# Convolution taps as scaled copies on ScalarE, summed in whole tiles, and one more seven-product unit pair in the first panel pair of two down parts

## The chip, the cores and the metric

The kernel runs on one core of a Trainium2 chip. The metric is the device time of one execution in microseconds: 2241.81 us is the median of three runs before the change (2240.89 to 2243.47). A core has TensorE (matmuls, with weight loads that overlap them), VectorE (DVE), ScalarE (ACT) and GpSimd (POOL) for arithmetic, SyncE (SP), which here only issues transfers, and 16 DMA engines. Each engine works through its own list of instructions in the order written.

## The reference, cut to what matters

The model is a two-layer trunk on 256 tokens of width 2048. Each layer has an attention part and a channel mixer; the change lies in the mixer, a gated MLP with a causal depthwise convolution of width 3 between the up-projection and the activation:

```python
def causal_dwconv(u, w, b):
    s_ = u.shape[1]
    up = jnp.pad(u, ((0, 0), (CONV_WIDTH - 1, 0), (0, 0)))
    return w[0] * up[:, 0:s_] + w[1] * up[:, 1:s_ + 1] + w[2] * up[:, 2:s_ + 2] + b

def conv_ffn(h, w_up, conv_w, conv_b, w_down):
    u = causal_dwconv(h @ w_up, conv_w, conv_b)
    a, val = split_cols(u, [FFN_HIDDEN, FFN_HIDDEN])
    return (jax.nn.silu(a) * val) @ w_down
```

FFN_HIDDEN is 5632, so `w_up` is 2048 x 11264 and `w_down` 5632 x 2048.

## The kernel before, in words

**Products.** Every float32 operand is split into a high part that TensorE takes at full pace (type fp32r) and a low part, the rest. A product is then three matmuls: high x high, low x high (both with the high weights, `whi`) and high x low (`wlo`). Weights arrive in units of 128 x 1024 words: two row blocks of 128 (chunks) by 512 output columns. `split_unit` loads a unit on SyncE's queue into `raw` (four buffers), casts it on ScalarE to `whi` (L208, three buffers) and subtracts on VectorE to get `wlo` (L217, three buffers). A plain unit is 12 matmuls: two token blocks of 128, two chunks, three each.

**Panels.** A panel is 512 output columns. `proj_tm` runs one panel through all its units, `proj_two` two panels. Evacuation copies the sums from PSUM, which has four accumulator banks.

**Seven products.** `proj_seven` takes two panels at a time. For a unit pair (the same two chunks in both panels) listed in its `forms` it computes the 2 x 2 block product with seven block products in place of eight, 21 matmuls in place of 24. It needs sums of the weight blocks, made on VectorE as they arrive (L346 to L349, then casts L314 and subtractions L315), and sums of the activation blocks, the `forms` tiles, made by `token_sums` (L400 to L406). Unit pairs that are not listed run as plain ones.

**The mixer.** The hidden width is worked through in three parts of 16, 16 and 12 chunks (`PARTS`). In each part up panels come first: one panel gives two chunks of the gate and two of the value, so a part has 8, 8 and 6 panels. Then the down-projection multiplies the part's chunks by `w_down` and adds to `x`. In the first two parts it runs as two panel pairs through `proj_seven`, each with eight unit pairs. `SEVEN` lists their seven-product places, counted from 0: (3, 5) in the first pair and (3, 5, 7) in the second. The last part has none: `proj_two`, then two `proj_tm`.

**The convolution.** An up panel's sums leave PSUM through ScalarE (L1116) token by token. VectorE transposes squares (L438), a write to DRAM and four reads back on ScalarE's queue (L446) bring them into `u` as channel by token, with two zero columns in front. `taken(j, base, u, i)` then handles half i of the panel, one gate and one value chunk of 128 x 256: ScalarE starts each with the last tap and the bias (L1092), VectorE adds the two other taps (L1093, L1094), ScalarE applies Silu (L1096), VectorE multiplies (L1097), and `split` makes the high and low parts in `m` (L523, L524), which the down-projection reads. For the panels whose chunks are a seven-product unit pair, `summed` makes the token sums.

**Order.** The steps after an evacuation are hung on the units that follow: `later((3, write), (6, read), (8, taken 0), (9, taken 1))` counts `split_unit` calls (in a seven-product unit pair, its two `passed()` calls), and each step is issued after the newest cast. For the second panel of a layer the last two counts are two higher. Loads, casts and subtractions of weights carry a higher priority than the rest (`AHEAD`); within these bounds a planner with a model of the instructions' times writes the order for each engine.

**Last panel.** The last up panel of a part gives the chunks of the last unit of the down panels. Its steps run while the down-projection is already under way.

Of the kernel before, what the change touches and what calls it, by code (L numbers as in the profile page):

```python
# [12 lines left out]
F32 = mybir.dt.float32  # L13
F32R = mybir.dt.float32r
I32 = mybir.dt.int32
AF = mybir.ActivationFunctionType
ALU = mybir.AluOpType
PSUM = bass.MemoryType.PSUM

P = 128  # L20
T = 256
# [10 lines left out]
PARTS = ((0, 16), (16, 32), (32, 44))  # L32
# [4 lines left out]
NVER = 96  # L37
NUNIT = 1024
AHEAD = 300
SEVEN = ((3, 5), (3, 5, 7))  # L40
LAST = ()

SPREAD = [128 * q + 32 * k + i for k in range(4) for i in range(32) for q in range(4)]
# [94 lines left out]
def _trunk(ctx: ExitStack, tc: tile.TileContext, xt, xtok, memt, wp, wgu, gns, gfin, cnv, par, msk, out):  # L138
    nc = tc.nc
    where, _ = _layout()  # L140
    V, S, TE = nc.vector, nc.scalar, nc.tensor
# [36 lines left out]
    def later(*steps):  # L178

        for units, step in steps:  # L180
            due.append([units, step])
# [242 lines left out]
    def natural(v):  # L424
        return v.rearrange("p (t h) -> p t h", h=2)
# [23 lines left out]
    def back():  # L449
        return tp.tile([P, 4, T], F32, name="back", tag="back", bufs=2)  # L450
# [65 lines left out]
    def split(dst, i, src, g=None, dealt=True):  # L516

        hi, lo = dst[i][:, 0, :], dst[i][:, 1, :]
        if dealt:
            hi, lo = (v.rearrange("p (h t) -> p h t", h=2) for v in (hi, lo))  # L520
            src = src.rearrange("p (t h) -> p h t", h=2)
        if g is None:
            S.activation(hi, src, AF.Copy)  # L523
            V.tensor_tensor(lo, src, hi.bitcast(F32), ALU.subtract)  # L524
        else:
            S.activation(hi, src, AF.Copy, scale=g)
            V.scalar_tensor_tensor(lo, src, g, hi.bitcast(F32), ALU.mult, ALU.subtract)  # L527
# [535 lines left out]
    def ffn(l, nx, h, m, then, ending=None):  # L1063
        with tc.tile_pool(name=f"ffn{l}", bufs=1) as fp, ExitStack() as ends:
# [3 lines left out]
            sp = sums.enter_context(tc.tile_pool(name=f"sums{l}", bufs=1))  # L1068
            cw = fp.tile([P, 4 * 88], F32, name="cw")
            nc.sync.dma_start(cw, cnv[l])  # L1070
            us = [fp.tile([P, 4, T + 2], F32, name=f"u{i}") for i in range(2)]
            for u in us:
                nc.gpsimd.memset(u[:, :, :2], 0.0)
            turn = [0]
            tiles = [sp.tile([P, 2, 4, P], F32R, name=f"forms{i}") for i in range(3)]
            held = []

            def spare_tile(name, dtype):
# [2 lines left out]
            def form(t):  # L1081
                return lambda i: [t[:, h, i, :] for h in range(2)]

            def taken(j, base, u, i):

                cv = []
                for c in range(2):
                    v = u[:, 2 * c + i, :]
                    col = (c * 44 + j + i) * 4
                    w = [cw[:, col + n : col + n + 1] for n in range(4)]  # L1090
                    r = fp.tile([P, T], F32, name=f"cv{c}", tag=f"cv{c}", bufs=3)
                    S.activation(r, v[:, 2:], AF.Identity, bias=w[3], scale=w[2])  # L1092
                    V.scalar_tensor_tensor(r, v[:, 1 : T + 1], w[1], r, ALU.mult, ALU.add)  # L1093
                    V.scalar_tensor_tensor(r, v[:, :T], w[0], r, ALU.mult, ALU.add)  # L1094
                    cv.append(r)
                S.activation(cv[0], cv[0], AF.Silu)  # L1096
                V.tensor_tensor(cv[1], cv[0], cv[1], ALU.mult)  # L1097
                split(m, j + i - base, cv[1])
                if (j - base) // 2 in parts[base]:
                    held.append(cv[1])  # L1100
                    if i:
                        summed(parts[base][(j - base) // 2])

            def summed(form):
                ab = [natural(h)[:, :, b] for h in held for b in range(2)]
                held.clear()
                token_sums(*ab, sp.tile([P, 4, P], F32, name="sf", tag="sf"), [form[:, h, :, :] for h in range(2)])

            def panel(j, base, slack=0):
                held = []  # L1110

                def evac(b, a):
                    if not held:
                        held.append(Turn("turned"))
                    e = tp.tile([P, 512], F32, name="scaled", tag="scaled", bufs=2)
                    S.activation(e, a, AF.Copy, scale=nx.col()[:, b : b + 1])  # L1116
                    held[0].put(b, e)
                    if not b:
                        return
                    u = us[turn[0] % 2]  # L1120
                    turn[0] += 1
                    later((3, held[0].write), (6, lambda: held[0].read(lambda k: u[:, k, 2:])),
                          (8 + slack, lambda: taken(j, base, u, 0)), (9 + slack, lambda: taken(j, base, u, 1)))

                return evac

            parts = {lo: dict(zip(SEVEN[1] if p < len(PARTS) - 1 else LAST, tiles)) for p, (lo, _) in enumerate(PARTS)}
            for p, (lo, hi) in enumerate(PARTS):
                forms = parts[lo]
                js = list(range(lo, hi, 2))  # L1130
# [6 lines left out]
                if p < len(PARTS) - 1:  # L1137
                    for f, at in zip((0, 2), SEVEN):
                        add_seven(key, f, m, {u: form(forms[u]) for u in at}, spare_tile)
# [33 lines left out]
    n, then, _ = preparing("ffn0", bufB)  # L1173
# [4 lines left out]
    n, then, _ = preparing("ffn1", bufA)  # L1178
# [132 lines left out]
```

## Time and profile before

| | value |
|---|---|
| median of three runs | 2241.81 us (2240.89 to 2243.47) |
| span of the profiled execution | 2241.1 us |
| TensorE busy | 2227.2 us, 99%, 10267 matmuls |
| VectorE busy | 1658.5 us, 74% |
| ScalarE busy | 1294.0 us, 58% |
| DMA | 516.98 MB, mean 231 GB/s |
| granted TensorE clock | 0.999 |

The page and the views come from one execution, taken by the hardware profiler; the span is the time from its first to its last instruction, and the page gives no other time for that execution. The timed runs are others. Busy time of TensorE includes the overlap of neighbouring matmuls (a 128 x 512 one is shown with about 0.39 us though one starts every 0.227 us in the mixer), so its share says that it hardly pauses, and the pace is read from starts. Views used: the page, the list of what each engine waited for, groups of instructions by line and shape (busy us, mean ns of one, then idle time before them and what ended it), busy time by stretch, and instructions in order of time (start us, duration us, engine, line, count).

### The profile page before, as it was taken

The page shows a single profiled execution, that of the slowest core. Times are in us where ns is not written, and L with a number is a line of the kernel's source. Part 1 is how long each engine was busy: PE and PEld are TensorE (multiplying, and loading weights), DVE is VectorE, ACT ScalarE, POOL GpSimd, SP SyncE. Part 2 cuts the span into 40 slices and gives each one's busy share as a digit, 9 for nine tenths or more (in the row PEclk, how much of TensorE's full clock was granted, in tenths as well). Part 3 has the DMA queues.
Part 4 walks back from the last instruction along what each step waited for, and adds up shares of the span by engine and source line. Part 5 has one row for each costly group of instructions (what it writes and reads, how often), then busy time and mean ns, then how long its engine had stood idle before and what let it go on. Part 6 is the DMA issues. An engine that isn't in the chain of part 4 may idle for free.

```text
span 2241.1 us, 29637 instructions
## 1 busy us (share of the span) xinstructions
PE 2227.2 (99%) x10267; PEld 1860.8 (83%) x10267; DVE 1658.5 (74%) x2608; ACT 1294.0 (58%) x1921; POOL 44.6 (2%) x71
## 2 busy tenths in 40 slices
PE   9999999999999999999999999999999999999998
PEld 7888888888888888888888898888888888888886
DVE  7568887667689677886777875666778967787766
ACT  7555665656565465555656655555665555554654
POOL 0000000000000000000000000000000000000000
PEclk9999999999999999999999999999999999999999
DMA  9875667677875778667778777677876677767784
GB/s 319 277 234 188 205 208 224 202 234 242 256 222 201 243 233 249 213 203 246 235 254 263 243 239 222 196 233 244 255 243 220 204 239 244 240 193 233 237 242 150
DMA packets 276894, 516.98 MB, mean 231 GB/s; under 512 B 149884, under 2 KB 158600, under 8 KB 276616
## 3 DMA queue, kind: packets, MB, share of 16 engines
q1 hardware_dynamic: 124296, 427.24, 58.9%
q10 hardware_dynamic: 149760, 80.51, 12.6%
q0 software_dynamic: 2688, 7.34, 1.1%
q8 instruction: 80, 1.31, 0.2%
q14 instruction: 70, 0.57, 0.1%
HBM read 470.44 MB, written 44.58 MB: 230 GB/s over the span
## 4 chain that ended last, share of the span: by engine, by line
PE 95%; DMA 3%; DVE 1%; issue 1%; ACT 0%; SPq 0%; DVEq 0%; ACTq 0%
PE acc L229 24%; PE acc L230 24%; PE acc L233 24%; PE acc L291 16%; PE ps_s L291 1%; DMA back<-xturned 1%; PE ps_o L291 1%; PE ps_t L291 1%; DMA back<-turned 1%; DMA raw<-wp 1%; PE ps_s L833 0%; DMA turned<-square 0%; PE ps_s L634 0%; PE ps_t L623 0%; PE ps_o L645 0%
## 5 line engine op out<-in xcount | busy, mean ns | idle before, releaser
L217 DVE TENSOR_TENSOR wlo<-raw,whi 128x1024 fp32r<-128x1024 f32 (+4 forms) x763 | 912.6, 1199 | 458.0 <-ACT whi L208 429.5
L208 ACT ACTIVATE whi<-raw 128x1024 fp32r<-128x1024 f32 (+4 forms) x763 | 791.2, 1040 | 704.7 <-PE acc L230 471.9
L229 PE MATMUL acc<-whi,B 128*128 128x512 f32 (+3 forms) x1440 | 548.1, 382 | 0.0
L230 PE MATMUL acc<-whi,B 128*128 128x512 f32 (+3 forms) x1440 | 547.9, 382 | 0.0
L229 PE MATMUL acc<-whi,A 128*128 128x512 f32 x1120 | 437.3, 392 | 1.7 <-ACT whi L208 1.4
L230 PE MATMUL acc<-whi,A 128*128 128x512 f32 x1120 | 435.4, 390 | 0.0
L233 PE MATMUL acc<-wlo,B 128*128 128x512 f32 (+3 forms) x1440 | 377.0, 381 | 0.0
L229 PEld LDWEIGHTS acc<-whi,B 128*128 128x128 f32 x1440 | 270.3, 188 | 46.9
L230 PEld LDWEIGHTS acc<-whi,B 128*128 128x128 f32 x1440 | 269.9, 188 | 46.3
L233 PEld LDWEIGHTS acc<-wlo,B 128*128 128x128 f32 x1440 | 267.7, 188 | 46.4
L233 PE MATMUL acc<-wlo,A 128*128 128x512 f32 x1120 | 300.6, 390 | 0.3 <-DVE wlo L217 0.3
L229 PEld LDWEIGHTS acc<-whi,A 128*128 128x128 f32 x1120 | 210.3, 188 | 48.1 <-ACT whi L208 3.6
L233 PEld LDWEIGHTS acc<-wlo,A 128*128 128x128 f32 x1120 | 210.1, 188 | 44.3 <-DVE wlo L217 0.7
L230 PEld LDWEIGHTS acc<-whi,A 128*128 128x128 f32 x1120 | 210.3, 188 | 43.5 <-DVE A L527 0.2
L291 PE MATMUL acc<-whi,B 128*128 128x512 f32 x508 | 132.2, 390 | 0.0
L291 PE MATMUL acc<-whi,A 128*128 128x512 f32 x496 | 129.9, 390 | 0.0
L291 PEld LDWEIGHTS acc<-whi,B 128*128 128x128 f32 x508 | 95.1, 188 | 20.3
L1092 ACT ACTIVATE cv<-u,cw 128x256 f32<-128x256 f32 x176 | 96.8, 588 | 23.9 <-DMA u<-turned 23.9
L291 PEld LDWEIGHTS acc<-whi,A 128*128 128x128 f32 x496 | 93.1, 188 | 19.9
L314 ACT ACTIVATE whi<-t 128x1024 fp32r<-128x1024 f32 x46 | 48.9, 1062 | 79.2 <-DVE t L349 42.7
L1093 DVE SCALAR_TENSOR_TENSOR cv<-u,cw,cv 128x256 f32<-128x256 f32 x176 | 78.5, 479 | 15.6 <-ACT cv L1092 15.6
L438 DVE STREAM_TRANSPOSE square<-scaled 128x512 f32<-128x512 f32 x122 | 80.3, 692 | 0.0
(259 smaller groups left out, 1819.5 us busy)
## 6 DMA issues: line engine op xcount, KB each, us to landing
raw<-wp SPq DMA_DIRECT2D x743, 512.0 KB, 4.2
turned<-square ACTq DMA_DIRECT2D x61, 512.0 KB, 4.5
u<-turned ACTq DMA_DIRECT2D x176, 128.0 KB, 5.2
raw<-wp SPq DMA_DIRECT2D x32, 384.0 KB, 3.2
raw<-wp SPq DMA_DIRECT2D x24, 388.0 KB, 3.9
xturned<-square ACTq DMA_DIRECT2D x12, 512.0 KB, 4.3
back<-xturned ACTq DMA_DIRECT2D x40, 128.0 KB, 5.6
raw<-wp SPq DMA_DIRECT2D x8, 400.0 KB, 3.8
```

The lines of the kernel that those rows point to most:

```text
L208: casts.append(S.activation(hi[:, s], raw[:, s], AF.Copy))
L217: V.tensor_tensor(lo[:, s], raw[:, s], hi[:, s].bitcast(F32), ALU.subtract)
L229: TE.matmul(acc[:, :n], xh, hi[:, s], start=first and j == 0, stop=False)
L230: TE.matmul(acc[:, :n], xl, hi[:, s], start=False, stop=False)
L233: TE.matmul(a, xh, ls, start=False, stop=stop)
L291: TE.matmul(a[:, :n], x, w, start=k not in begun, stop=calls[k] == 0)
L314: casts.append(S.activation(hi, raw, AF.Copy))
L438: V.transpose(self.square[:, :, :, b], src.rearrange("p (c t) -> p c t", t=32))
L1092: S.activation(r, v[:, 2:], AF.Identity, bias=w[3], scale=w[2])
L1093: V.scalar_tensor_tensor(r, v[:, 1 : T + 1], w[1], r, ALU.mult, ALU.add)
```

## The change

`SEVEN` becomes ((1, 3, 5), (3, 5, 7)): the first panel pair of parts 0 and 1, in both layers, computes the unit pair at place 1 with seven products too. There are four tiles of token sums in place of three (`SUMS` = 1, 3, 5, 7).

The convolution is handled for a whole panel at a time. A panel is one tile of 128 x 4 x 256: two gate chunks, two value chunks. `begun` (at the former count of `taken` for half 0) has ScalarE write last tap plus bias into tile `a` and the middle tap, a copy scaled per channel, into tile `b`, four instructions each; VectorE adds them as one 128 x 1024 addition. `taken` (at the former count of half 1) writes the first tap into `b`, four copies again, adds the tiles, applies Silu to both gate chunks in one instruction, multiplies in one instruction, and splits the two chunks as before. The tiles come from the pool entry `back`, which has two buffers; the `cv` tiles are gone. The multiply-adds of VectorE (L1093, L1094) are replaced by eight more ScalarE copies and two additions per panel.

```diff
-SEVEN = ((3, 5), (3, 5, 7))
+SEVEN = ((1, 3, 5), (3, 5, 7))
+SUMS = (1, 3, 5, 7)
...
-            def taken(j, base, u, i):
-
-                cv = []
+            def taps(t, u, j, n):
+
                 for c in range(2):
-                    v = u[:, 2 * c + i, :]
-                    col = (c * 44 + j + i) * 4
-                    w = [cw[:, col + n : col + n + 1] for n in range(4)]
-                    r = fp.tile([P, T], F32, name=f"cv{c}", tag=f"cv{c}", bufs=3)
-                    S.activation(r, v[:, 2:], AF.Identity, bias=w[3], scale=w[2])
-                    V.scalar_tensor_tensor(r, v[:, 1 : T + 1], w[1], r, ALU.mult, ALU.add)
-                    V.scalar_tensor_tensor(r, v[:, :T], w[0], r, ALU.mult, ALU.add)
-                    cv.append(r)
-                S.activation(cv[0], cv[0], AF.Silu)
-                V.tensor_tensor(cv[1], cv[0], cv[1], ALU.mult)
-                split(m, j + i - base, cv[1])
-                if (j - base) // 2 in parts[base]:
-                    held.append(cv[1])
-                    if i:
-                        summed(parts[base][(j - base) // 2])
+                    for i in range(2):
+                        k = 2 * c + i
+                        col = (c * 44 + j + i) * 4
+                        g = [cw[:, col + m : col + m + 1] for m in range(4)]
+                        if n == 2:
+                            S.activation(t[:, k, :], u[:, k, 2:], AF.Identity, bias=g[3], scale=g[2])
+                        else:
+                            S.activation(t[:, k, :], u[:, k, n : T + n], AF.Copy, scale=g[n])
+
+            def begun(j, u, got):
+                a, b = back(), back()
+                got += [a, b]
+                taps(a, u, j, 2)
+                taps(b, u, j, 1)
+                V.tensor_tensor(a, a, b, ALU.add)
+
+            def taken(j, base, u, got):
+                a, b = got
+                taps(b, u, j, 0)
+                V.tensor_tensor(a, a, b, ALU.add)
+                S.activation(a[:, :2, :], a[:, :2, :], AF.Silu)
+                V.tensor_tensor(a[:, 2:, :], a[:, :2, :], a[:, 2:, :], ALU.mult)
+                for i in range(2):
+                    split(m, j + i - base, a[:, 2 + i, :])
+                u = (j - base) // 2
+                if u in parts[base]:
+                    held.extend(a[:, 2 + i, :] for i in range(2))
+                    summed(parts[base][u])
...
                     later((3, held[0].write), (6, lambda: held[0].read(lambda k: u[:, k, 2:])),
-                          (8 + slack, lambda: taken(j, base, u, 0)), (9 + slack, lambda: taken(j, base, u, 1)))
+                          (8 + slack, lambda: begun(j, u, got)), (9 + slack, lambda: taken(j, base, u, got)))
```

More of the change, by code (lines that the diff above doesn't have):

```diff
@@ L1074, in ffn @@
             turn = [0]
-            tiles = [sp.tile([P, 2, 4, P], F32R, name=f"forms{i}") for i in range(3)]
+            tiles = [sp.tile([P, 2, 4, P], F32R, name=f"forms{i}") for i in range(len(SUMS))]
             held = []
@@ L1119, in evac @@
                         return
-                    u = us[turn[0] % 2]
+                    u, got = us[turn[0] % 2], []
                     turn[0] += 1
                     later((3, held[0].write), (6, lambda: held[0].read(lambda k: u[:, k, 2:])),
-                          (8 + slack, lambda: taken(j, base, u, 0)), (9 + slack, lambda: taken(j, base, u, 1)))
+                          (8 + slack, lambda: begun(j, u, got)), (9 + slack, lambda: taken(j, base, u, got)))
                 return evac
-            parts = {lo: dict(zip(SEVEN[1] if p < len(PARTS) - 1 else LAST, tiles)) for p, (lo, _) in enumerate(PARTS)}
+            parts = {lo: dict(zip(SUMS if p < len(PARTS) - 1 else LAST, tiles)) for p, (lo, _) in enumerate(PARTS)}
             for p, (lo, hi) in enumerate(PARTS):
```

## The prediction

> **What bounds the kernel now.** I read the page first (span, busy shares, chain of waits), then what TensorE waits for, then the pace of its matmuls in the chain listed in order of time.
>
> ```profile
> span 2241.1 us, 29637 instructions
> PE 2227.2 (99%) x10267; PEld 1860.8 (83%) x10267; DVE 1658.5 (74%) x2608; ACT 1294.0 (58%) x1921; POOL 44.6 (2%) x71
> PE 95%; DMA 3%; DVE 1%; issue 1%; ACT 0%; SPq 0%; DVEq 0%; ACTq 0%
> ...
> PE ps_o L174 <- DVE B L171: 1.5, 1, 1.5
> PE acc L229 <- ACT whi L208: 1.4, 3, 0.7
> PE ps_s L634 <- DMA back<-turned: 1.1, 2, 0.8
> PE acc L233 <- DVE wlo L217: 0.3, 1, 0.3
> PE acc L229 <- ACT A L526: 0.2, 1, 0.2
> ...
> 643.41 16.32 PE acc L291 x72
> 661.80 1.40 PE ps_s L291 x6
> ```
>
> The first three rows say TensorE. The next five (what waited <- for what: us in total, times, longest) say that all its waits together are 4.5 us, none at L291, the line of the seven-product panels. So in the mixer time is a number of matmuls times their pace, and a change of VectorE or ScalarE work is worth nothing until TensorE has to wait. The last two rows give the pace: 16.32 / 72 = 0.2267 us for matmuls on plain activations, 1.40 / 6 = 0.233 us for those whose activations are a tile of token sums.
>
> The covers come next: one up panel of part 1, then the first and the second down pair of part 0. The columns are the stretch, its length, busy us (x instructions) of TensorE, weight loads, VectorE, ScalarE and GpSimd, the granted clock, the DMA share and GB/s.
>
> ```profile
> 771.40:793.20 21.80, 21.80 (x98) 18.06 (x97) 15.30 (x22) 12.91 (x20) 0.00 (x0) 1.00 0.80 243
> 643.40:685.60 42.20, 42.20 (x187) 34.71 (x186) 34.82 (x51) 25.53 (x33) 0.00 (x0) 1.00 0.70 221
> 685.60:727.00 41.40, 41.40 (x183) 34.01 (x182) 38.05 (x46) 21.02 (x23) 0.00 (x0) 1.00 0.58 194
> ```
>
> The granted clock is 1.00 in each. VectorE has 7.4 us free in the first pair and 3.4 us in the second, which already has three seven-product unit pairs and the evacuation of the first pair, and in which TensorE does not wait either.
>
> **The change, part by part.** *The added unit pairs.* The first down pair of parts 0 and 1 gets one more in both layers: four in all. A plain unit pair is 2 units x 12 matmuls = 24 x 0.2267 = 5.44 us. A seven-product one is 21, of which 12 use token sums: 9 x 0.2267 + 12 x 0.233 = 4.84 us. Gain 0.60 us each, **2.4 us** for four, all on the path that sets the end. The bytes loaded stay the same.
>
> What it adds elsewhere is priced by these groups (busy us, mean ns of one):
>
> ```profile
> L217 DVE TENSOR_TENSOR wlo<-raw,whi 128x1024 fp32r<-128x1024 f32 x697 | 850.0, 1222 | 415.5 <-ACT whi L208 393.1 <-PE acc L291 11.5 <-PE acc L233 4.0
> L208 ACT ACTIVATE whi<-raw 128x1024 fp32r<-128x1024 f32 x697 | 735.4, 1058 | 638.8 <-PE acc L230 422.3 <-issue 60.1 <-PE acc L291 47.9
> L346 DVE TENSOR_TENSOR t<-raw 128x512 f32<-128x512 f32 x23 | 15.9, 691 | 9.5 <-DMA raw<-wp 9.3
> L314 ACT ACTIVATE vhi<-raw 128x512 fp32r<-128x512 f32 x23 | 14.5, 628 | 18.4 <-DMA raw<-wp 13.4 <-DVE t L346 4.9
> L1092 ACT ACTIVATE cv<-u,cw 128x256 f32<-128x256 f32 x176 | 96.8, 588 | 23.9 <-DMA u<-turned 23.9
> L1093 DVE SCALAR_TENSOR_TENSOR cv<-u,cw,cv 128x256 f32<-128x256 f32 x176 | 78.5, 479 | 15.6 <-ACT cv L1092 15.6
> L1097 DVE TENSOR_TENSOR cv<-cv,cv 128x256 f32<-128x256 f32 x88 | 36.9, 419 | 1.4 <-ACT cv L1096 1.4
> L1096 ACT ACTIVATE cv<-cv 128x256 f32<-128x256 f32 x88 | 35.8, 406 | 1.7 <-DVE cv L1094 1.5
> L526 ACT ACTIVATE A<-back,gains 128x256 fp32r<-128x256 f32 x32 | 15.2, 515 | 6.2 <-DMA back<-xturned 6.2
> ```
>
> On VectorE a plain unit pair takes two subtractions, 2.44 us; a seven-product one takes 3 x 1.22 + 5 x 0.69 = 7.1 us, 4.7 us more. The first pair has 7.4 us free, so this lies beside TensorE; without that cover it would cost up to 4.7 us at each of four places. ScalarE casts 3 x 1.06 + 0.63 in place of 2 x 1.06, 1.7 us more, with 16.7 us free. The new sums tile is made long before, in the up panels.
>
> *The convolution.* For each of 44 panel pairs VectorE loses eight tap instructions (8 x 0.479) and two products (2 x 0.419), 4.67 us, and gets two whole-tile additions (2 x 1.22) and one product over 512 columns (0.69), 3.13 us: 1.5 us less. ScalarE gets eight scaled copies. The trace has no such copy from u; the nearest is L526, same shape with a per-partition scale, 0.515 us: 4.1 us more, less 0.2 us because two Silu of 0.406 become one of about 0.63. In an up panel ScalarE goes from 12.9 to about 16.8 of 21.8 us and VectorE from 15.3 to 13.8. Over the run that is 1294 + 44 x 3.9 + 9, about 1475 us on ScalarE (66%). Neither fills up, so the amount costs **0**.
>
> [...]
>
> *Buffers.* The two whole tiles replace the cv tiles and are written again a panel (21.8 us) later; only the first two panels of a layer stand closer, and their results are first read six panels on. Writes and reads of u keep their queue and place. Cost 0.
>
> *What the copies stand in front of.* They are queued on ScalarE with the weight casts, and behind a cast stand VectorE's subtraction and TensorE's products. Part 2's down of layer 0 shows how far casts run ahead:
>
> ```profile
> 1116.49 0.39 PE L229 MATMUL acc<-whi,A 128*128 128x512 f32 x1
> ...
> 1130.09 0.39 PE L229 MATMUL acc<-whi,A 128*128 128x512 f32 x1
> ...
> 1138.25 0.39 PE L229 MATMUL acc<-whi,A 128*128 128x512 f32 x1
> ...
> 1143.69 0.39 PE L229 MATMUL acc<-whi,A 128*128 128x512 f32 x1
> ...
> 1144.14 0.62 PE L229 MATMUL acc<-whi,A 128*128 128x512 f32 x2
> ...
> 1129.38 1.06 ACT L208 ACTIVATE whi<-raw 128x1024 fp32r<-128x1024 f32 x1 [1.66 <-PE acc L230]
> 1130.35 1.08 ACT L1092 ACTIVATE cv<-u,cw 128x256 f32<-128x256 f32 x2
> 1132.10 1.06 ACT L208 ACTIVATE whi<-raw 128x1024 fp32r<-128x1024 f32 x1 [0.67 <-PE acc L230]
> ...
> 1139.83 0.42 DVE L524 TENSOR_TENSOR A<-cv,A 128x256 fp32r<-128x256 f32 x1
> ```
>
> With three buffers the cast at 1132.10 is freed by the unit that began at 1130.09 and serves the one that begins at 1138.25: it has 1138.25 - 1132.10 - 1.06 = 5.1 us of cover. A whole burst of taps is 4 x 0.588 + 4 x 0.515 less about 0.1 us of overlap each (two taps in 1.08 us), 3.7 us. So even a burst wholly ahead of a cast is hidden. Cost 0; without the cover, up to 3.7 us a panel.
>
> *The longer chain: what is late next.* The last up panel of a part feeds the last unit of the down panels. Eleven units of 2.72 us separate them in part 2: the first down product is at 1116.49, the one that needs this panel at 1143.69, and the last half of it is ready at 1139.83 + 0.42 = 1140.25. That leaves 3.4 us. The old chain took 9.9 us from its first tap at 1130.35, with both halves overlapping; in the new one the engines take turns, since the second tile is written again for tap 0 only after the first addition has read it. From 1130.35: four taps 2.1, the waiting cast 1.0, four copies 1.8, addition 1.2, four copies 1.8, addition 1.2, Silu 0.6, product 0.7, two splits 0.8 and 0.4. If casts and subtractions fall between the steps, the last half is ready near 1142.5 and nothing waits. If each that is ready goes first (one cast more in the second four copies, one before the split, a subtraction before the second addition, before the product and before the split), the first half comes at 1144.4 and the last at 1145.9. TensorE would then lose 0.7 us, or 1.9 us if it also waits for the low parts. Bounds 0 to 1.9 at each of two places. I take 0.35, half of the first lateness, because ready casts do go ahead of taps in the rows above; **+0.7 us** for two.
>
> In the first pair of parts 0 and 1 the same chain serves the plain unit pair at the last place:
>
> ```profile
> 659.88 1.08 ACT L1092 ACTIVATE cv<-u,cw 128x256 f32<-128x256 f32 x2
> ...
> 677.54 0.42 DVE L524 TENSOR_TENSOR A<-cv,A 128x256 fp32r<-128x256 f32 x1
> ```
>
> That pair of panels ends at 643.41 + 6 x 5.44 + 2 x 4.84 = 685.7, so its last 24 products start about 680.3, and 0.6 us earlier after the change: 1.7 us of cover behind 677.96. The chain here is long (18 us) because VectorE's high-priority subtractions go first, and it has less to do on VectorE now; if it grew as in part 2 (2.2 to 5.7 us), 0.5 to 4.0 us would be lost at each of four places. I take **0**, since ScalarE is idle for 16.7 us there and the second pair shows 38.05 us of VectorE work in 41.40 us without a wait; a gain is excluded, as there is no wait to remove.
>
> *Sum.* -2.4 + 0 + 0.7 + 0 = -1.7 us: a span of 2239.4 us from 2241.1. The median of the runs, 2241.81 us, lies 0.7 us above the span, so **2240.1 us**.
>
> **The rivals.** *The chain eats the gain*: at both part-2 places all 1.9 us are lost, 3.8 in place of 0.7: 2241.81 - 2.4 + 3.8 = 2243.2 us. For it: 3.4 us of cover against a chain with seven hand-overs between engines. Against it: the two matmuls of L229 in a row at 1144.14 show that products are already issued out of their plain order, what is ready first.
>
> *Slower*: the last panel's convolution in the first pair comes late at the last unit pair. Place: four first pairs; price: mean growth (2.2 + 5.7) / 2 - 1.7 = 2.2 us each, 8.9 us: 2241.81 - 2.4 + 0.7 + 8.9 = 2249.0 us. It decides once the four lose 6.2 us together, 1.55 us each. For it: VectorE's new 4.7 us stand ahead of it, each step waits for subtractions, and the last half now ends only 2.3 us before use. Against it: VectorE has 7.4 us free and 1.5 us less per panel.
>
> *ScalarE holds casts behind taps that wait for their transfer.* One step now needs all four blocks of u where it needed two.
>
> ```profile
> 524.72 0.60 ACT L1092 ACTIVATE cv<-u,cw 128x256 f32<-128x256 f32 x1 [2.97 <-DMA u<-turned]
> ```
>
> For it: such a wait of 2.97 us and a burst of 3.7 us pass the cover of 5.1 us by 1.6 us; at four panels the time is 2241.81 - 2.4 + 0.7 + 6.4 = 2246.5 us. Against it: the row of L1092 has 23.9 us of these waits in all, about 0.5 us a panel. [...]
>
> *Faster*: the shifted plan also removes waits outside the mixer. At most 4.5 us exist, of which 1.5 are at the start: 2241.81 - 2.4 - 3.0 = 2236.4 us.
>
> *No effect*: the third unit pair is delayed by its loads and gives back its 2.4 us: 2241.8 us.
>
> **How the numbers follow.** Forecast 0.56 (own range 2239.0 to 2241.2, from no lateness to the first lateness at both places), gain eaten 0.20, slower 0.10, casts held 0.06 (half past the bound), faster 0.04, no effect 0.04. A measurement can tell 0.2%, 4.5 us, from no change: below 2237.3 or above 2246.3. That gives faster 0.04, slower 0.10 + 0.03 = 0.13, same 0.83. The range goes from 2238.4 (no lateness, less the spread of about 1 us in the runs) to 2244.5 (gain eaten, plus the same).
>
> **What would show it.** 12 matmuls fewer, 10255; at L291 10 x 24 + 6 x 21 = 366 instead of 369 in each of the four downs, about 0.6 us shorter from first to last. L1093 and L1094 gone; ScalarE near 1475 us, VectorE near 1615 us (-44 x 1.5 + 4 x 4.7 and the new sums). TensorE's waits in the mixer under 1 us but for some tenths at the last unit of part 2's down. I am wrong if waits of microseconds stand at L291 or in part 2, or if the up panels (21.8 us each) grow.

## The result, and the profile after

The changed kernel is slower. Its median is 2254.93 us (four runs, 2253.48 to 2262.46), beside 2242.64 us for the kernel before in the same comparison (2240.89 to 2244.32): a ratio of 1.0057, with a 95% interval of 1.0042 to 1.0072. The forecast was 2240.1 us, with a range up to 2244.5. The profiled execution has a span of 2252.0 us, 10.9 us more than before. The first rows of the page after:

```profile
span 2252.0 us, 29434 instructions
PE 2232.5 (99%) x10255; PEld 1858.9 (83%) x10255; DVE 1639.3 (73%) x2344; ACT 1430.5 (64%) x2241; POOL 44.7 (2%) x71
PE 80%; DMA 8%; DVE 5%; ACT 4%; issue 2%; ACTq 0%; SPq 0%; DVEq 0%
```

The 12 matmuls are gone (10255), as forecast. VectorE has less to do and ScalarE more, though neither by as much as forecast (1639.3 us for about 1615, 1430.5 us for about 1475). But the chain that ended last, 95% TensorE before, now runs through VectorE, ScalarE and transfers for 17%. What TensorE waited for after (what waited <- for what: us in total, times, longest):

```profile
PE acc L230 <- ACT whi L209: 2.7, 3, 1.9
PE acc L292 <- ACT whi L209: 2.4, 4, 0.6
PE ps_o L175 <- DVE B L172: 1.5, 1, 1.5
PE acc L292 <- DVE wlo L218: 1.1, 3, 0.5
```

Lines ahead of the convolution are one further down than before: L292 is the seven-product line L291. It had no wait before. This view counts from the modelled end of a matmul (0.39 us long, where one starts every 0.227 us), so each pause is longer than its row. I therefore laid the two traces side by side by starts of matmuls, with a "down part" reaching from the first to the last start at the seven-product line (parts 0 and 1 of both layers, 84.04 to 84.08 us each before):

| stretch | after minus before, us |
|---|---|
| four down parts | +2.33, +1.12, +1.63, +1.13 = +6.2 |
| from the second layer's attention up to its first down part | +3.4, with one pause of 2.3 us |
| part 2 of the first layer and what follows it | +0.9 |
| all up panels of part 1 (174.3 us each) | 0.0 |
| the rest | +0.4 |

The four down parts should be 2.4 us shorter in all, since 12 matmuls are gone. They hold 8.6 us of lost time that no view of before has, all of it in the first panel pairs: the second pairs are as long as before to within 0.1 us. One of the pauses, in the second layer's part 1 (instructions in order of time: start us, us, engine, line, operation, count, and in brackets the idle time before):

```profile
1979.78 1.04 ACT L209 ACTIVATE whi<-raw 128x1024 fp32r<-128x1024 f32 x1
1980.73 2.06 ACT L1093 ACTIVATE back<-u,cw 128x256 f32<-128x256 f32 x4
1982.70 1.69 ACT L1095 ACTIVATE back<-u,cw 128x256 f32<-128x256 f32 x4
1984.30 1.04 ACT L209 ACTIVATE whi<-raw 128x1024 fp32r<-128x1024 f32 x1
...
1983.73 1.08 PE L292 MATMUL acc<-wlo,B 128*128 128x512 f32 x4
1985.39 2.14 PE L292 MATMUL acc<-whi,B 128*128 128x512 f32 x8 [0.58 <-ACT whi L209]
```

Eight taps stand in one unbroken run on ScalarE between two weight casts, 1980.73 to 1984.30. TensorE starts its last product at 1983.73 + 3 x 0.227 = 1984.41 and the next at 1985.39, when the cast behind the taps is done: 0.98 us between starts, 0.75 us lost. The same pause, behind the same eight taps, stands 23.6 to 24.7 us into each of the four down parts, with 0.97 to 0.99 us between starts. The four take 3.0 of the 8.6 us. The rest lies in shorter pauses, at the start of the pairs and behind this one, of up to 0.93 us between starts; the longer of them end with a low part of weights or with a cast in a seven-product unit pair.

The second reading is by stretches of 4 us around the start of that down part, which is at 1951.10 us before and at 1960.81 us after. Columns as in the prediction's windows: stretch, length, busy us of TensorE, weight loads, VectorE, ScalarE, GpSimd, granted clock, DMA share, GB/s. Before:

```profile
1947.10:1951.10 4.00, 4.00 (x20) 3.30 (x18) 3.90 (x9) 2.56 (x5) 0.00 (x0) 1.00 0.50 172
1951.10:1955.10 4.00, 4.00 (x19) 3.34 (x18) 3.57 (x5) 2.94 (x5) 0.00 (x0) 1.00 0.72 222
1955.10:1959.10 4.00, 4.00 (x20) 3.30 (x19) 0.88 (x2) 2.07 (x2) 0.00 (x0) 1.00 0.84 296
...
1971.10:1975.10 4.00, 4.00 (x19) 3.29 (x18) 4.00 (x8) 3.17 (x5) 0.00 (x0) 1.00 0.25 68
1975.10:1979.10 4.00, 4.00 (x19) 3.29 (x18) 4.00 (x7) 2.16 (x3) 0.00 (x0) 1.00 0.77 238
1979.10:1983.10 4.00, 4.00 (x19) 3.26 (x18) 4.00 (x7) 3.30 (x6) 0.00 (x0) 1.00 0.58 219
```

And after:

```profile
1956.80:1960.80 4.00, 4.00 (x19) 3.31 (x18) 2.12 (x3) 4.00 (x8) 0.00 (x0) 1.00 0.29 115
1960.80:1964.80 4.00, 4.00 (x18) 3.00 (x17) 4.00 (x6) 4.00 (x9) 0.00 (x0) 1.00 0.35 101
1964.80:1968.80 4.00, 4.00 (x19) 3.26 (x18) 4.00 (x6) 2.62 (x3) 0.00 (x0) 1.00 0.93 299
...
1980.80:1984.80 4.00, 4.00 (x18) 2.93 (x16) 2.72 (x5) 4.00 (x10) 0.00 (x0) 1.00 0.70 253
1984.80:1988.80 4.00, 3.37 (x14) 2.47 (x14) 3.96 (x6) 4.00 (x7) 0.00 (x0) 1.00 0.08 30
```

Two things are to be seen. Before, VectorE is full from 20 to 32 us into the pair, where most of the last panel's convolution stands. What it has free lies elsewhere: 3.1 us in one early stretch (4 - 0.88), about 2.4 us in the last 10 us, the rest mostly between 12 and 20 us. After, ScalarE is full for 8 us around the pair's start, mostly with taps, and VectorE waits for them in the first half of that. It is then full for 16 us; in the stretch of the pause it waits 1.28 us for a load of weights.

### The profile page after: what moved, and what is told of

The parts are those of the page before. It is cut to its first block, busy times and chain, and to the rows that moved or that the text cites. A ratio compares the mean times of both kernels' runs of the same rounds, so it can differ in the third digit from the quotient of the medians.

```text
span 2252.0 us, 29434 instructions
## 1 busy us (share of the span) xinstructions
PE 2232.5 (99%) x10255; PEld 1858.9 (83%) x10255; DVE 1639.3 (73%) x2344; ACT 1430.5 (64%) x2241; POOL 44.7 (2%) x71
## 4 chain that ended last, share of the span: by engine, by line
PE 80%; DMA 8%; DVE 5%; ACT 4%; issue 2%; ACTq 0%; SPq 0%; DVEq 0%
PE acc L230 21%; PE acc L231 21%; PE acc L234 21%; PE acc L292 11%; DMA u<-turned 3%; DMA turned<-square 3%; DVE wlo L218 2%; ACT back L1095 1%; DMA raw<-wp 1%; PE ps_s L292 1%; ACT whi L209 1%; ACT back L1093 1%; DVE wlo L316 1%; PE ps_o L292 1%; DMA xturned<-square 1%
## 5 line engine op out<-in xcount | busy, mean ns | idle before, releaser
L218 DVE TENSOR_TENSOR wlo<-raw,whi 128x1024 fp32r<-128x1024 f32 (+4 forms) x755 | 898.4, 1198 | 374.6 <-ACT whi L209 339.9
L209 ACT ACTIVATE whi<-raw 128x1024 fp32r<-128x1024 f32 (+4 forms) x755 | 777.5, 1037 | 549.4 <-PE acc L231 364.1
L1095 ACT ACTIVATE back<-u,cw 128x256 f32<-128x256 f32 x352 | 150.7, 494 | 0.0
L1102 DVE TENSOR_TENSOR back<-back 128x1024 f32<-128x1024 f32 x44 | 53.9, 1225 | 122.2 <-ACT back L1095 122.2
L292 PE MATMUL acc<-whi,B 128*128 128x512 f32 x484 | 127.9, 392 | 1.2 <-ACT whi L209 1.2
L292 PE MATMUL acc<-whi,A 128*128 128x512 f32 x472 | 125.6, 391 | 1.2 <-ACT whi L209 1.2
L1093 ACT ACTIVATE back<-u,cw 128x256 f32<-128x256 f32 x176 | 96.8, 593 | 31.5 <-DMA u<-turned 31.1
L292 PEld LDWEIGHTS acc<-whi,B 128*128 128x128 f32 x484 | 90.5, 188 | 21.3 <-ACT whi L209 2.0
L292 PEld LDWEIGHTS acc<-whi,A 128*128 128x128 f32 x472 | 88.3, 188 | 21.3 <-ACT whi L209 2.5
L315 ACT ACTIVATE whi<-t 128x1024 fp32r<-128x1024 f32 x54 | 57.2, 1059 | 71.3 <-DVE t L350 41.4
```

The costliest lines, as they stand in the source:

```text
L209: casts.append(S.activation(hi[:, s], raw[:, s], AF.Copy))
L218: V.tensor_tensor(lo[:, s], raw[:, s], hi[:, s].bitcast(F32), ALU.subtract)
L292: TE.matmul(a[:, :n], x, w, start=k not in begun, stop=calls[k] == 0)
L315: casts.append(S.activation(hi, raw, AF.Copy))
L1093: S.activation(t[:, k, :], u[:, k, 2:], AF.Identity, bias=g[3], scale=g[2])
L1095: S.activation(t[:, k, :], u[:, k, n : T + n], AF.Copy, scale=g[n])
```

## The experiments

The table goes ahead of the single runs. Ratios are to the kernel before, run beside it on the same chip, with the 95% interval. "Down parts" is the change of the four stretches above in the profiled execution; -2.4 is what four more seven-product pairs would give without pauses. What was expected of each run, as put on record before it, stands in its group. Theories A, B and C are defined in the text on seven_only, theory D in the one on all_spread. "Half clock" counts the stretches of 3.4 us ahead of the last matmul in which TensorE's granted clock fell to 0.50 (last section). A single profiled execution can lie some us from its kernel's median: where the two speak differently, the ratio decides.

| run | places, first pair | convolution | ratio (95%) | span | down parts | half clock |
|---|---|---|---|---|---|---|
| the change | 1, 3, 5 | new | 1.0057 (1.0042 to 1.0072) | 2252.0 | +6.2 | 1 |
| conv_only | 3, 5 | new | 1.0042 (1.0027 to 1.0056) | 2254.5 | +10.2 | 0 |
| seven_only | 1, 3, 5 | old | 1.0054 (1.0034 to 1.0073) | 2262.8 | +18.1 | 3 |
| old_last | 1, 3, 5 | new, last panel of a part old | 1.0100 (1.0084 to 1.0115) | 2266.5 | +20.1 | 2 |
| spread | 1, 3, 5 | as old_last, taps in three steps | 1.0090 (1.0075 to 1.0105) | 2259.8 | +16.8 | 1 |
| conv_spread | 3, 5 | new, taps in three steps | 1.0028 (1.0015 to 1.0041) | 2242.9 | +0.7 | 0 |
| all_spread | 1, 3, 5 | new, taps in three steps | 1.0041 (1.0027 to 1.0054) | 2254.3 | +6.6 | 1 |
| late_spread | 1, 3, 5 | all_spread, one unit later | 1.0063 (1.0046 to 1.0080) | 2245.9 | +5.3 | 0 |
| own_raw | 1, 3, 5 | new | 1.0072 (1.0057 to 1.0087) | 2258.2 | +10.9 | 0 |
| own_raw_seven | 1, 3, 5 | old | 1.0042 (1.0027 to 1.0057) | 2242.7 | +3.2 | 0 |
| seven_lean | 1, 3, 5 | old | 1.0069 (1.0054 to 1.0084) | 2259.0 | +15.1 | 3 |
| seven_notaps | 1, 3, 5 | old, less in the last panel | 1.0001 (0.9991 to 1.0010) | 2241.4 | -0.3 | 0 |
| place6 | 3, 5, 6 | as all_spread | 1.0124 (1.0109 to 1.0139) | 2273.4 | +27.5 | 5 |
| place246 | 2, 4, 6 | as all_spread | 1.0058 (1.0040 to 1.0076) | 2251.4 | +5.5 | 0 |
| relief1 | 1, 3, 5 | new in the last panel alone, three steps | 1.0036 (1.0027 to 1.0046) | 2248.3 | +6.5 | 0 |
| relief246 | 2, 4, 6 in both pairs | as relief1 | 1.0042 (1.0027 to 1.0057) | 2253.1 | +10.0 | 0 |

No version is faster than the kernel before.

### Which part costs: conv_only, seven_only

conv_only takes the new convolution and leaves the places; seven_only is the kernel before with these lines alone:

```diff
-SEVEN = ((3, 5), (3, 5, 7))
+SEVEN = ((1, 3, 5), (3, 5, 7))
+SUMS = (1, 3, 5, 7)
```

> The changed kernel with the seven-product places of before, (3, 5) and (3, 5, 7); the convolution is the new one. Theory A: all the lateness is here, and the 2.4 us of the matmuls are missing: about 2.4 us above the changed kernel, ratio to the kernel before 1.006 to 1.007. Theory B: at or below the time of before, ratio 0.998 to 1.001, since VectorE has 68 us less. Theory C: as A.

> The kernel before with the third seven-product unit pair in the first down pair of parts 0 and 1; the convolution stays as before, with taps on ScalarE two at a time. Theory A (bursts: eight taps in a row on ScalarE stand in front of a weight cast, and TensorE waits for the cast): no bursts here, so only the gain of 12 matmuls remains, about 2.4 us below the kernel before, ratio 0.999. Theory B (VectorE: the 4.7 us of work that the third unit pair adds is what comes late): the loss is here too, ratio 1.003 or more. Theory C (ScalarE: the 172 us added to it are too many, in whatever order): as A.

Each part alone makes the kernel slower. conv_only has 10.2 us of pauses in the down parts, nearly all of it waits for casts; what TensorE waited for there:

```profile
PE acc L292 <- ACT whi L209: 7.2, 7, 1.7
```

seven_only has 18.1 + 2.4 = 20.5 us lost there, nearly all at the products of weight sums and the plain unit that follows:

```profile
PE ps_o L292 <- ACT whi L315: 4.2, 4, 1.0
PE acc L292 <- ACT whi L209: 4.0, 3, 2.2
...
PE ps_s L292 <- DVE wlo L316: 3.2, 3, 1.1
```

The two parts do not add. In the down parts of the profiled executions they lose 20.5 + 10.2 = 30.7 us apart and 8.6 us together. The ratios say it more weakly: 1.0054 and 1.0042 apart, 1.0057 together, with intervals that overlap, where a sum would be 1.0096. The reason that fits is that the new convolution takes work from VectorE, which is what the third unit pair lacks; old_last and relief1 below bear on it. So the cost of the change is not the sum of two costs, and both of my zeros were wrong, each for a reason of its own.

### The burst of taps: conv_spread, all_spread, late_spread

In place of eight taps and then four, all panels but the last of a layer (`j == 42`) write four taps in each of three steps:

```diff
-                          (8 + slack, lambda: begun(j, u, got)), (9 + slack, lambda: taken(j, base, u, got)))
+                          (8 + slack, lambda: begun(j, u, got)),
+                          ((8 if j == 42 else 9) + slack, lambda: second(u, j, got)),
+                          ((9 if j == 42 else 10) + slack, lambda: taken(j, base, u, got)))
```

conv_spread does this to conv_only, all_spread to the change; late_spread puts all steps of all_spread one unit later, but for the last panel of a part.

> conv_only with the taps in three steps of four at three successive units (two steps for the last panel of a layer, as in the changed kernel), so that no eight taps stand between two casts but in two places. Same work on every engine, same 10267 matmuls. Theory A (bursts): the pauses of conv_only about 21 us into the four first down pairs, where TensorE waits for the cast, are gone: 6 us or more below conv_only, ratio to the kernel before 1.000 to 1.002. If the copies are too much whatever their order: ratio 1.003 to 1.005 as conv_only.

> The changed kernel with the same spreading, the third unit pair included. Theory A alone: all pauses of the mixer gone, ratio 0.999 to 1.001. Theory A with theory D (the third unit pair holds two of the four raw buffers until VectorE has made its sums, so the next loads start late): the pauses about 24 us into the first down pairs are gone, pauses near the seven-product places stay, ratio 1.002 to 1.005.

> all_spread with the taps of all panels but the last of each part one unit later, so that the reads of u have 2.7 us more to land before a tap stands first on ScalarE. If taps that wait for u hold up the casts (the 3.5 us and 3.6 us waits and TensorE's 3.9 us pause before the first down pair of the second layer in all_spread), those pauses go: 3 us or more below all_spread, ratio 1.001 to 1.003. If only place 1 matters: as all_spread, 1.004.

In conv_spread the pauses of the down parts go from 10.2 to 0.7 us, with the same instructions in a different order. What is left of TensorE's waits at the seven-product line, where conv_only has 7.2 us in seven waits:

```profile
PE acc L292 <- ACT whi L209: 0.5, 1, 0.5
```

That shows the burst as the cause in the down parts of these two executions. It does not bring the kernel back: the median of conv_spread stays 0.28% above before, outside the 1.000 to 1.002 that was expected, with an interval that overlaps that of conv_only, and its profiled execution was the fastest of six, so where the others lose their time is not seen. all_spread gains little over the change (1.0041 against 1.0057, intervals that overlap): the pauses about 24 us into the pairs are gone, and others, mostly of 0.6 to 0.8 us between starts, stand 10 to 16 us into them. late_spread, expected at 1.001 to 1.003, gains nothing (1.0063), though the long pause shown next is absent from its profiled execution, the fastest of four.

all_spread shows the third cost of taps that stand ahead of casts, that of waiting for their own data:

```profile
1688.85 1.04 ACT L209 ACTIVATE whi<-raw 128x1024 fp32r<-128x1024 f32 x1
1693.53 1.91 ACT L1093 ACTIVATE back<-u,cw 128x256 f32<-128x256 f32 x3 [3.64 <-DMA u<-turned]
1698.93 0.60 ACT L1093 ACTIVATE back<-u,cw 128x256 f32<-128x256 f32 x1 [3.49 <-DMA u<-turned]
1699.43 1.04 ACT L209 ACTIVATE whi<-raw 128x1024 fp32r<-128x1024 f32 x1
...
1700.53 3.06 PE L292 MATMUL acc<-whi,B 128*128 128x512 f32 x8 [3.88 <-ACT whi L209]
```

ScalarE stands twice for a transfer of `u`, with casts written behind the taps, and TensorE loses 3.88 us at one place. The changed kernel has a smaller case, a wait of 3.68 us ahead of the taps and a pause of TensorE of 0.60 us behind them:

```profile
616.77 2.13 ACT L1093 ACTIVATE back<-u,cw 128x256 f32<-128x256 f32 x4 [3.68 <-DMA u<-turned]
...
621.50 0.50 PE L230 MATMUL acc<-whi,B 128*128 128x512 f32 x1 [0.60 <-ACT whi L209]
```

### What the third unit pair lacks: seven_lean, seven_notaps, own_raw_seven, own_raw

All but own_raw start from seven_only. seven_lean leaves out the four weight sums of VectorE at place 1, seven_notaps the multiply-adds of VectorE in the last up panel of parts 0 and 1:

```diff
-                    V.scalar_tensor_tensor(r, v[:, 1 : T + 1], w[1], r, ALU.mult, ALU.add)
-                    V.scalar_tensor_tensor(r, v[:, :T], w[0], r, ALU.mult, ALU.add)
+                    if j not in (14, 30):
+                        V.scalar_tensor_tensor(r, v[:, 1 : T + 1], w[1], r, ALU.mult, ALU.add)
+                        V.scalar_tensor_tensor(r, v[:, :T], w[0], r, ALU.mult, ALU.add)
```

own_raw_seven gives the first unit of each seven-product pair in the mixer a buffer of its own, so that the four of `raw` come free sooner; own_raw does this to the change:

```diff
-                r0, r1 = (load(units[i][u]) for i in range(2))
+                r0, r1 = (load(units[i][u], tiles("r0", F32) if own and not i else None) for i in range(2))
```

> seven_only without the four weight-sum instructions of VectorE at place 1 (the raw units are used in place of their sums, so the output of these unit pairs is not the reference's): 2.75 us of VectorE and the steps that casts wait for are gone at each of four places, the 12 matmuls less stay. If VectorE at place 1 is what comes late in seven_only, its pauses there (18 us over the four first down pairs, with the 2.4 us gained 20 us) shrink to 8 us or less and the ratio is 0.999 to 1.002. If the cause is the casts, the loads or what stands around place 1, it stays near 1.005.

> seven_only without the eight multiply-adds of VectorE in the last panel of parts 0 and 1 (their output is then not the reference's): 3.8 us of VectorE less at each of the four first down pairs, right where its list has no gap (places 3 to 5). If VectorE is late there, TensorE's pauses about 30 us into these pairs (3 us each in seven_only and seven_lean) go; those near place 1 (1 to 2.6 us) stay: ratio 0.999 to 1.003. If raw buffers or loads are the cause: 1.005 as seven_only.

> seven_only with a buffer of its own for the first raw unit of each seven-product unit pair in the mixer. If the raw buffers are the cause (loads after place 1 start late: ScalarE waits 3.8 us for one there), the pauses near place 1 and place 5 shrink by half or more: ratio 1.000 to 1.003. If VectorE is the cause: 1.005 as seven_only, with the pauses about 30 us into the pairs unchanged.

> The changed kernel; in the mixer the first raw unit of each seven-product unit pair is loaded into a buffer of its own, so that three or four of the common raw buffers stay free for the plain units behind it. Theory D: pauses of TensorE in the down pairs that follow late loads are gone; those from eight taps before a cast stay: 2 to 4 us below the changed kernel. Theory A alone: no change, ratio 1.005 to 1.006.

seven_lean loses the pauses at place 1 and behind it, but those at the end of place 5, which end 30 to 33 us into the pair, stay, and the time does too (1.0069). seven_notaps, which takes eight multiply-adds of 0.48 us out of VectorE at one place of each of the four pairs, brings nearly all of it back: the ratio is 1.0001, where 2.4 us gained would give 0.999. Three of the four down parts are 0.2 to 0.65 us shorter than before, about as the matmuls left out should make them; the fourth is 1.1 us longer, with a pause near place 1 and one at place 5. The place is seen in seven_only in order of time (part 1 of the first layer, VectorE, then TensorE):

```profile
933.53 0.47 DVE L1095 SCALAR_TENSOR_TENSOR cv<-u,cw,cv 128x256 f32<-128x256 f32 x1
933.93 1.22 DVE L316 TENSOR_TENSOR wlo<-raw,whi 128x1024 fp32r<-128x1024 f32 x1
935.07 0.68 DVE L349 TENSOR_TENSOR t<-raw,t 128x512 f32<-128x512 f32 x1
935.67 0.41 DVE L1098 TENSOR_TENSOR cv<-cv,cv 128x256 f32<-128x256 f32 x1
936.00 0.47 DVE L1095 SCALAR_TENSOR_TENSOR cv<-u,cw,cv 128x256 f32<-128x256 f32 x1
936.40 1.21 DVE L316 TENSOR_TENSOR wlo<-t,whi 128x1024 fp32r<-128x1024 f32 x1
937.53 0.68 DVE L350 TENSOR_TENSOR t<-raw,t 128x512 f32<-128x512 f32 x1
...
937.67 0.73 PE L292 MATMUL ps_s<-wlo,forms 128*128 128x512 f32 x2 [1.05 <-DVE wlo L316]
939.44 0.50 PE L292 MATMUL ps_o<-whi,forms 128*128 128x512 f32 x1 [1.04 <-ACT whi L315]
```

VectorE goes without a gap from the convolution (L1095, L1098) to the weight sums (L349, L350) and back. TensorE starts at 937.67, as the subtraction of 936.40 ends, and at 939.44 behind the cast of the sum that L350 made. In the 4 us that begin 28 us into this pair TensorE gets 11 matmuls done, 19 in seven_notaps. VectorE is full in both: what differs is that in seven_only it is behind with what TensorE needs next. The stretch in seven_only:

```profile
934.60:938.60 4.00, 2.75 (x11) 1.61 (x9) 4.00 (x8) 0.70 (x2) 0.00 (x0) 1.00 0.67 240
```

And in seven_notaps:

```profile
927.20:931.20 4.00, 4.00 (x19) 3.19 (x18) 4.00 (x7) 3.65 (x4) 0.00 (x0) 1.00 0.64 216
```

Buffers are a part of it, since a unit that waits for VectorE keeps its raw tile: own_raw_seven has smaller pauses at place 5 and none at place 1 (+3.2 in place of +18.1 in its profile, the fastest execution of five), though with runs from 2244.5 to 2257.5 us its median is still 0.42% above before. Added to the change the same buffer does not help: 1.0072 against 1.0057.

### The last panel and the places: old_last, spread, relief1, place6, place246, relief246

old_last puts the old convolution back into the last panel of each part of the change, spread does the same with the others in three steps; relief1 is the reverse of old_last, the old convolution in all panels but the last of parts 0 and 1:

```diff
+                          *((8, lambda: halves_of(j, base, u, 0)), (9, lambda: halves_of(j, base, u, 1)))
+                          if j + 2 in (16, 32, 44) else
+                          ((8 + slack, lambda: begun(j, u, got)), (9 + slack, lambda: taken(j, base, u, got))))
```

> The changed kernel, but the last up panel of each part is convolved as before, half by half with multiply-adds on VectorE; the other 38 panels keep the new way. Theory A: the pauses of about 1 us inside the four first down pairs, some 23.6 us after their start, are gone, and the one in part 2's down too; pauses in the first up panels of a layer and at the very start of the down pairs stay: 4 to 6 us below the changed kernel, ratio 1.003 to 1.004. Theory C: 6 of 44 panels relieved, a seventh of the loss, ratio 1.005.

> As old_last, but the other 38 panels make their taps in three steps of four at three successive units (last tap, middle tap with the addition, first tap with the rest) in place of eight and four at two: no run of more than four taps stands between two weight casts. ScalarE has the same work. Theory A: TensorE's pauses in the mixer are gone; what is left is the gain of 12 matmuls and whatever else happened in the second layer's attention: ratio 0.999 to 1.001. Theory C: as old_last, ratio 1.003 to 1.005.

> seven_only with the new convolution, in three steps of four taps, for the last panel of parts 0 and 1 alone: VectorE is relieved between places 3 and 5, ScalarE is not loaded anywhere else. VectorE theory: the pauses about 30 us into the first down pairs go, those at place 1 stay: ratio 1.000 to 1.003, 4 us or more below seven_only. Loads theory: 1.005.

If the new convolution's longer chain were what hurts in the first pair, old_last would be better than the change. It is worse, 1.0100 where 1.003 to 1.004 was expected, with 20.1 us in the down parts: the copies on ScalarE spare VectorE exactly where it is full. spread, expected at 0.999 to 1.001, is no better (1.0090). In both the tiles of the old convolution have two buffers, where before has three; that was not tried by itself. relief1 keeps just that relief and has the lowest ratio of those with a third pair that compute everything (1.0036, with an interval that overlaps others), but pauses stay at place 4, now for VectorE's low parts:

```profile
PE acc L292 <- DVE wlo L218: 4.6, 4, 1.5
```

place6, place246 and relief246 move the third pair, with the edits in `SEVEN` that the table gives:

> all_spread with the third unit pair at place 6 in place of 1: (3, 5, 6). Same number of matmuls and the same VectorE work. If the trouble is the neighbourhood of the up panels (their last convolutions, evacuations and transfers beside a seven-product unit pair), the pauses near the start of the first down pairs go; but 5, 6 and the last panel's chain for place 7 stand close: pauses may come at places 6 and 7. Ratio 0.999 to 1.001 if only the neighbourhood matters, 1.003 or more if three unit pairs are too many for this panel pair wherever they stand.

> all_spread with the three unit pairs at (2, 4, 6): one place further from the up panels, with a plain unit pair between each two. If the neighbourhood of the up panels is the trouble: ratio 0.999 to 1.001. If not: 1.003 or more.

> relief1 with the places (2, 4, 6) in both panel pairs: three unit pairs in the first, as in the changed kernel, three in the second. The seven-product pairs stand one place further from the up panels. If place 1 and the last panel's convolution were the whole trouble: no pauses, 12 matmuls less, ratio 0.999 to 1.000, the one version below the kernel before. If pauses appear elsewhere: 1.002 or more.

place6 is the worst kernel of all, with 27.5 us: two seven-product pairs stand in a row, whose 2 x 7.1 us on VectorE (the prediction's price) face 2 x 4.84 us of TensorE; that reason was not tried by itself, and in two of the four pairs a pause near the start takes 2.6 us as well. Places 2, 4, 6 bring no gain over 1, 3, 5 in either form. None of the sets tried finds 4.7 us of VectorE free where it needs them.

### The pause in the second layer's attention: before_again

Some 183 us behind the last seven-product panel of the second layer's attention, the change has one pause of TensorE of 2.3 us between starts, behind ScalarE's queue:

```profile
1495.68 0.37 ACTq L447 DMA_DIRECT2D back<-xturned  x1
1496.45 1.06 ACT L209 ACTIVATE whi<-raw 128x1024 fp32r<-128x1024 f32 x1 [6.68 <-PE acc L234]
```

The issue of a read at 1495.68 waits for a write that lands late (8.2 us after its issue at 1487.39, where the same write takes 6.1 us in before), and the cast is queued behind it. That the queue holds the cast, and not TensorE, which the row names, is read from this order in time and was not tried. before_again runs the kernel before unchanged once more.

> The kernel before, a second profile. All five kernels made from it paused 1.3 to 2.3 us in the second layer's attention, about 183 us after its last seven-product pair, and the kernel before did not. If that pause is a matter of how transfers happen to fall, it can be here too; if it belongs to the new orders written by the planner, it is absent.

Its span is 2241.4 us and it has no such pause; nor has own_raw_seven, where the write takes 6.6 us. All other versions have one there, of 0.8 to 2.5 us between starts. The change does not touch these instructions. Why the write lands late in nearly all versions and not in before is open.

## Why the prediction was wrong

**"On VectorE ... The first pair has 7.4 us free, so this lies beside TensorE"**: this step failed, and it is the larger. 7.4 us is a difference of sums over 42.2 us. The rows by 4 us show 3.1 us of it in one early stretch and none from 20 to 32 us into the pair, where the sums of place 5 and most of the last panel's convolution stand. The text named the price without cover (up to 4.7 us at each of four places, 18.8 us) and then took zero; seven_only lost 20.5 us there, some 5 of them through the clock (below), and the relief of VectorE at that one place (seven_notaps) took nearly all of it away. The second pair, which has three places and 38.05 us of VectorE work without a wait, was a false witness: no panel's convolution stands in it.

**"So even a burst wholly ahead of a cast is hidden. Cost 0"**: this step failed too. The cover of 5.1 us was read at one cast of part 2, between plain units. The burst's length was right, 3.6 us for 3.7. But in the plain unit pair behind a seven-product one (place 4) the weights of the late cast landed only at 1981.0, and TensorE was free for them at 1984.64: at most 1984.64 - 1981.0 - 1.04 = 2.6 us of cover. TensorE lost 0.75 us there in the change and up to 1.9 us in conv_only. In conv_spread, which has the same taps in shorter runs, the down parts lose 0.7 us in place of 10.2.

**A term that was missing**: the sum has none for the attention, and it gives no reason for that. The profiled execution lost 3.4 us between the second layer's attention and its first down part, 2.1 of them in the one pause. Why is open.

**The gain of 0.60 us a pair** was right: it shows in seven_notaps, where three of four down parts are shorter. In the change it is eaten by pauses of 8.6 us.

**The slower rival** gave 2249.0 us with 8.9 us lost in the four first pairs, and 8.6 us were lost there in the profiled execution. But its mechanism, the last panel's chain late at the last unit pair, did not occur: no pause stands at place 7, they stand at the start and at places 4 and 5. Its size was right by chance. **Casts held behind taps that wait for their transfer**, a rival with 0.06, did happen at 616.77 (0.60 us) and in all_spread (3.88 us). It is a part of the loss, not the whole.

**The chain in part 2** was priced at 0.35 us a layer with a bound of 1.9. One pause of 0.65 us between starts stands there in the first layer, none in the second: 0.4 us lost at TensorE's pace for 0.7 forecast. Right. The up panels of part 1 did not grow, as forecast.

**The amounts.** ScalarE was forecast near 1475 us and came to 1430.5, mostly because copies overlap: the row below has 0.494 us of one (0.515 in the prediction), but four take 1.69 us (1982.70).

```profile
L1095 ACT ACTIVATE back<-u,cw 128x256 f32<-128x256 f32 x352 | 150.7, 494 | 0.0
```

VectorE was forecast near 1615 us and came to 1639.3: the sum took each instruction at its whole length, but here too the next one starts before the last has ended (in the rows of seven_only 0.40 us behind a multiply-add of 0.47, 1.14 behind a subtraction of 1.22), so that many short instructions weigh less than their lengths. Neither amount was the question; the order was.

**Readings that do not come out.** Ten units, not eleven, separate the two products of part 2 (27.20 / 2.72); the 3.4 us are read from times and stand. The steps listed for the new chain add up to 1141.95, not 1142.5, and how the later bound of 1144.4 and 1145.9 follows from them is not shown. The +0.7 us rests on that bound, and 0.4 us were measured.

**What stays open**: the late write in the second layer's attention (2.1 us of pause and 1.6 us through the clock), the shorter pauses of the change that no run took away, and the wider spread of the runs. The change runs from 2253.5 to 2262.5 us, conv_spread from 2245.0 to 2254.4, where the kernel before stays within 2240.9 to 2247.8 in all its runs. Only one execution of each was traced (two of the kernel before).

## What to carry to other kernels

Free time of an engine is to be read in stretches of a few microseconds (4 us here, in a stage of 42), at the place where the new work will stand; a mean over a stage says nothing of it. The longest unbroken run of other work written between two instructions that TensorE needs (here eight taps between two casts, 3.6 us) is the number to hold against the cover at that very place; the same work in shorter runs cost 0.7 us in place of 10.2 in the down parts. Two edits that load and relieve the same engine must be costed together and taken apart on the chip: here either alone lost more in the down parts than both together, and the ratio of both (1.0057) is well below what the two ratios would add up to (1.0096).

## What the runs showed of the hardware

**A pause and 3.4 us at half clock behind it.** I had reckoned a pause at its length. In the changed kernel, around the pause of 2.3 us in the second layer's attention (stretches of 3.4 us, columns as above):

```profile
1495.00:1498.40 3.40, 1.50 (x7) 0.90 (x7) 0.86 (x1) 1.95 (x4) 1.49 (x2) 1.00 0.50 156
1498.40:1501.80 3.40, 3.40 (x10) 2.64 (x9) 3.40 (x7) 3.40 (x6) 0.00 (x0) 0.50 0.82 232
1501.80:1505.00 3.20, 3.20 (x15) 2.62 (x14) 3.20 (x6) 2.83 (x5) 0.00 (x0) 1.00 0.80 202
```

Two matmuls of it in order of time:

```profile
1499.22 0.63 PE L231 MATMUL acc<-whi,B 128*128 128x512 f32 x1
1499.65 0.63 PE L230 MATMUL acc<-whi,B 128*128 128x512 f32 x1
```

The granted clock is 0.50 for the 3.4 us behind the pause, and matmuls start every 0.43 us in place of 0.227: some eight of them, about 1.6 us more. seven_only has three such stretches, one behind two pauses of only 1.05 and 1.04 us (TensorE 1.49 us busy in the first row, with granted clock 1.00; then 0.50):

```profile
936.80:940.20 3.40, 1.49 (x5) 0.96 (x6) 3.37 (x8) 1.87 (x2) 0.00 (x0) 1.00 0.72 229
940.20:943.60 3.40, 3.40 (x9) 2.59 (x9) 3.38 (x6) 2.89 (x5) 0.00 (x0) 0.50 0.39 118
```

In own_raw the pause in the attention was 2.4 us long and no stretch at 0.50 followed (granted clock 0.999 over that execution). What tells such a pause from the one of 2.3 us in the change is not shown.

At the 1.6 us measured for the stretch in the change, the counts of the table make about 5 of seven_only's 20.5 us (three stretches) and 8 us in place6 (five): an estimate.
